# A two-layer decoder segment on one core: the first normalisation is moved behind the projections, and x is also laid out transposed

## The chip, the cores and the metric

The kernel runs on one core of a Trainium2 chip. Its time is the device time of one execution in microseconds; the time before is the median of three runs, 907.67 (907.3 to 909.54). The engines are TensorE (PE; its weight loads are PEld), VectorE (DVE), ScalarE (ACT), GpSimd (POOL) and SyncE (SP, whose queue issues nearly all DMAs). Each engine works through its own instructions in a fixed order, and waits on semaphores for the others.

## The reference

Two layers over 1024 tokens of width 1024, batch 1, all in float32. Each layer is x <- x + RMSNorm(mixer(RMSNorm(x))):

```python
def rmsnorm(x, w):
    y = x * lax.rsqrt(jnp.mean(x * x, axis=-1, keepdims=True) + NORM_EPS)
    return y * w

h = rmsnorm(x, pre_norm_w[0])
proj = h @ w_in + b_in                       # 1024 x 2304: q 1024, k 128, v 128, z 1024
q, k = partial_rope(q, positions), partial_rope(k, positions)
o = sliding_window_gqa(q, k, v, sinks)       # 16 query heads, 2 key heads, window 128
x = x + rmsnorm((o * silu(z)) @ w_out + b_out, post_norm_w[0])
```

Layer 1 has a gated linear recurrence in place of the attention. The change touches only the first RMSNorm and the projections of layer 0. Since the norm's factor r[t] is one number per token, (x * r * w) @ W = r * ((x * w) @ W): the row factor can be applied after the product as well as before it.

## The kernel before

Products are exact to float32 by splitting: a matrix a is held as two fp32r tiles, hi (a rounded copy) and lo (a - hi), and a product is three matmuls, hi hi + hi lo + lo hi (`product`, L186). The tokens stand in two halves of 512, the model width in eight slices k of 128. `act[k, half]` is the pair (acth, actl), 128 x 512, of the transposed normalised input. The weights come in slots of 128 x 512 (`wraw`, 256 KB each, four buffers), are split into `whi` and `wlo` (ten pairs, and two of their own for the key weights, kw) and are freed after their last use.

A projection unit (`proj_feat`, L191) makes one 128-column group of the output for one half: eight k times three matmuls, 24 products of 128 x 512 into one PSUM bank. Layer 0 has units v, k, q (g, ct) and z, each for both halves. The eviction of a unit differs by kind: q is biased, partly rotated, split into qh and ql and stored to DRAM (`qd`), from which attention reads its blocks (`QS`); k is rotated by tables cosT, sinT, cosK and kept as KH, KL; v is transposed; z is gated into og.

The head. Before the branch (the `tc.If` on a flag that tells which form of the recurrence is safe) the first 512 rows of x are loaded as four tiles of 128 tokens, squared on ScalarE (L978), and their row factors made on GpSimd (`rstd_of`, L211). After the branch VectorE multiplies each row by its factor (`norm_rows`), TensorE transposes the result in 128 x 128 pieces (`transpose_half`, L233, four for each k, 32 in all), and ScalarE and VectorE take acth and actl out of PSUM (`act_from_psum`, L177). The second half goes the same way a little later, between the first units. `advance` (L137) splits the weights as slots come free: hi on GpSimd up to slot 19 and on ScalarE after, lo on VectorE, and for slots 2 and 3 on GpSimd.

Then come 16 attention blocks (g, b), into which the remaining units are woven as filler for TensorE by a table of counts (`fill`, `at`). At the end `g_split` splits o * silu(z) into act again, and the output projection `out0_first` follows.

What sets the order: the framework places instructions by priorities (`tc.high_priority`) and a schedule that it makes at build time; instructions of an engine wrapped in `InOrder` keep the order in which they are written. Before, only VectorE is wrapped, and only in the head. In a build's rows such instructions carry the line of `InOrder` (L87).

## Time and profile before

| what | value |
|---|---|
| median of three runs | 907.67 us |
| the profiled execution: its time, its span | 907.38 us, 905.7 us |
| TensorE busy | 883.6 us, 98% |
| VectorE, ScalarE, GpSimd busy | 556.7, 378.2, 330.6 us |
| products of layer 0's input projection that TensorE runs by 59.49 us | 168 |
| DMA moved | 78.63 MB |

The page gives the busy time of each engine, the groups of instructions by line, and the chain of work that ended last. Busy matmul times overlap (a product takes 0.39 us from start to end, while the next starts after 0.23), so TensorE's pace is read from the distance between starts. Views with a time window show single instructions; times are microseconds from the span's start.

### The profile page before, as it was taken

What the parts mean: (1) busy time and instruction counts of PE and PEld (TensorE: products, weight loads), DVE (VectorE), ACT (ScalarE), POOL (GpSimd) and SP (SyncE); (2) the same over time, 40 slices, a digit from 0 to 9 for tenths busy, and PEclk for the clock granted to TensorE, in tenths of its full rate; (3) what the DMA queues carried; (4) which work ended last, traced back from release to release, by engine and by line L of the source; (5) the groups of instructions that cost most, each with busy time, mean ns of one, the idle gap of its engine ahead of it and who ended that gap; (6) DMA issues with size and microseconds to landing.
All of it is one profiled execution on the core that took longest, in us unless ns stands there. A gap on an engine that the chain in (4) does not pass through costs nothing.

```text
span 905.7 us, 14367 instructions
## 1 busy us (share of the span) xinstructions
PE 883.6 (98%) x5342; PEld 738.6 (82%) x5342; DVE 556.7 (61%) x919; ACT 378.2 (42%) x982; POOL 330.6 (37%) x498
## 2 busy tenths in 40 slices
...
GB/s 284 159 146 184 105 184 128 154 56 76 85 37 81 81 93 138 172 122 42 87 50 34 25 47 1 69 58 28 35 47 47 1 1 93 1 110 78 24 185 121
DMA packets 53608, 78.63 MB, mean 87 GB/s; under 512 B 4824, under 2 KB 25048, under 8 KB 53528
## 3 DMA queue, kind: packets, MB, share of 16 engines
...
## 4 chain that ended last, share of the span: by engine, by line
PE 76%; DVE 8%; POOL 6%; issue 5%; ACT 2%; DMA 2%; SPq 0%; POOLq 0%; ACTq 0%; DVEq 0%
PE psmm L189 63%; POOL rstd L217 2%; PE psk L853 1%; PE pso L866 1%; PE pss L530 1%; PE pss L531 1%; PE pso L868 1%; PE pst L551 1%; POOL ms L215 1%; ACT sm L545 1%; DVE actl L180 1%; PE pst L847 1%; PE pst L880 1%; DMA o<-in_x 1%; PE psd L804 1%
## 5 line engine op out<-in xcount | busy, mean ns | idle before, releaser
L189 PE MATMUL psmm<-acth,whi 128*128 128x512 f32 x528 | 208.8, 396 | 0.6 <-DVE ql L378 0.3
L189 PE MATMUL psmm<-acth,wlo 128*128 128x512 f32 x528 | 207.8, 394 | 0.2 <-POOL wlo L155 0.2
L189 PE MATMUL psmm<-actl,whi 128*128 128x512 f32 x528 | 207.7, 393 | 0.0
L189 PE MATMUL psmm<-whi,acth 128*128 128x512 f32 (+1 forms) x520 | 202.7, 391 | 0.5 <-DVE y L632 0.5
L189 PE MATMUL psmm<-wlo,acth 128*128 128x512 f32 (+1 forms) x520 | 200.7, 387 | 0.0
L189 PE MATMUL psmm<-whi,actl 128*128 128x512 f32 (+1 forms) x520 | 200.6, 388 | 0.0
L155 DVE TENSOR_TENSOR wlo<-wraw,whi 128x512 fp32r<-128x512 f32 x126 | 94.8, 765 | 93.4 <-ACT whi L154 86.6
L189 PEld LDWEIGHTS psmm<-acth,whi 128*128 128x128 f32 x528 | 99.3, 188 | 20.9 <-DVE qf L706 0.8
L189 PEld LDWEIGHTS psmm<-acth,wlo 128*128 128x128 f32 x528 | 99.2, 188 | 19.9 <-POOL wlo L155 0.6
L189 PEld LDWEIGHTS psmm<-whi,acth 128*128 128x128 f32 x520 | 97.7, 188 | 20.4 <-DVE y L632 0.8
L189 PEld LDWEIGHTS psmm<-actl,whi 128*128 128x128 f32 x528 | 99.2, 188 | 18.2
L189 PEld LDWEIGHTS psmm<-whi,actl 128*128 128x128 f32 x520 | 97.7, 188 | 19.6
L189 PEld LDWEIGHTS psmm<-wlo,acth 128*128 128x128 f32 x520 | 97.8, 188 | 19.2
L154 ACT ACTIVATE whi<-wraw 128x512 fp32r<-128x512 f32 x112 | 70.2, 631 | 87.3 <-PE psmm L189 67.4
L545 ACT ACTIVATE sm<-sm,st 128x129 f32<-128x129 f32 x128 | 50.0, 393 | 56.0 <-DVE st L543 56.0
L714 POOL TENSOR_SCALAR gate<-gate,lbt 128x512 f32<-128x512 f32 x16 | 17.7, 1108 | 119.1 <-ACT gate L712 108.5
L927 DVE TENSOR_TENSOR y<-psmm,wpost 128x512 f32<-128x512 f32 (+1 forms) x17 | 11.2, 660 | 53.7 <-ACT jk L926 50.5
L217 POOL TENSOR_TENSOR rstd<-ms,nhalf 128x1 f32<-128x1 f32 (+1 forms) x48 | 41.7, 870 | 3.8
L562 POOL TENSOR_SCALAR_AFFINE_SELECT mY<-pT 64x256 fp32r<-64x256 f32 x56 | 28.6, 511 | 36.7 <-ACT pT L554 31.0
L926 ACT ACTIVATE jk<-psmm 128x512 f32<-128x512 f32 (+1 forms) x17 | 9.7, 571 | 67.0 <-PE psmm L189 67.0
L179 ACT ACTIVATE acth<-pst,cst 128x512 fp32r<-128x512 f32 x48 | 29.6, 693 | 12.7 <-PE pst L237 12.7
L565 POOL TENSOR_SCALAR_AFFINE_SELECT mY<-pT 64x256 fp32r<-64x256 f32 x64 | 31.8, 496 | 6.9 <-ACT pT L554 1.6
...
## 6 DMA issues: line engine op xcount, KB each, us to landing
wraw<-in_w SPq DMA_DIRECT2D x132, 256.0 KB
...
```

The source lines that it names most:

```text
L154: nc.scalar.activation(hi, raw, AF.Copy)
L155: W["split_ins"][i] = (nc.gpsimd if on_pool else v).tensor_tensor(lo, raw, hi.bitcast(F32), op=ALU.subtract)
L179: ins = nc.scalar.activation(hi, ps, AF.Copy, scale=scale)
L180: W["actl"][k] = v.scalar_tensor_tensor(lo, ps, scale, hi.bitcast(F32), op0=ALU.mult, op1=ALU.subtract)
L189: W["mm"] = nc.tensor.matmul(ps, a, b, start=(k == 0 and i == 0), stop=(k == NK - 1 and i == 2))
L217: W["rstd"] = keep(nc.gpsimd.tensor_tensor(r, m, nhalf[:, :width], op=ALU.pow))
L545: nc.scalar.activation(sm[:, h, :], sm[:, h, :], AF.Exp, bias=nm[:, h:h + 1], scale=0.125, accum_out=dn[:, h:h + 1])
L562: nc.gpsimd.affine_select(mY[r, :, :64], src[64:, :, :64].bitcast(F32), [[0, 4], [-1, 64]], ALU.is_gt, 0.0, base=0, channel_multiplier=1)
L565: nc.gpsimd.affine_select(mY[r, :, 64:], src[:64, :, 64:].bitcast(F32), [[0, 4], [1, 64]], ALU.is_ge, 0.0, base=0, channel_multiplier=-1)
L714: nc.gpsimd.tensor_scalar(dst, dst, ol, lb, op0=ALU.mult, op1=ALU.add)
L926: nc.scalar.activation(jk[:, c0:c1], ps, AF.Square, scale=D ** -0.5, accum_out=ss)
L927: v.tensor_tensor(y[:, c0:c1], ps, wpost[:, c * 512 + c0:c * 512 + c1], op=ALU.mult)
```

## The change

The host hands over x a second time, transposed (`xt`), so that a tile 128 x 512 of it is one slice k of one half as TensorE needs it.

First half. Each tile of xt is only multiplied by the norm's weight (a factor for each partition) and split: acth on ScalarE, actl on VectorE, both from SBUF. The row factors are left out of the products. The units of this half are therefore unscaled; every eviction of the first half begins with `scaled`: VectorE multiplies the PSUM bank by `rb0`, a 128 x 512 tile that holds the 512 row factors in every partition. `rb0` is made by `spread`: four 128 x 128 transposes of a factor column that is broadcast along the free axis, and a ScalarE copy. The factors come from squares of the ordinary rows of x, which are loaded for that alone, after the first tiles (into the space of the second half's tiles, and, for the second half's rows, of the tables cosT, sinT, cosK and kf/tK).

The first two units, v and q (0, 1), run side by side: for each k three products of the one and three of the other. Their weights (slots 0, 2, 1, 3 in this order) are loaded between the tiles of xt. Of slots 0 and 2 the first 128 columns are split on ScalarE, the rest on GpSimd; all lo parts are VectorE's.

Second half. Its tiles of xt are loaded after the rows of x, multiplied in place by `rb1` (the even k on GpSimd, the odd ones on VectorE), and then split like the others. So its units need no `scaled`.

All five engines are now wrapped in `InOrder` through the head. Further: the identity is made on GpSimd instead of loaded; the half-0 q units of group 0 keep qh and ql in the space of o0; the tag ql has one buffer where it had two; z's th moved to the tag qh.

How the order moves, at three places (names: whi_80 to whi_89 are the ten slots, acth_0_104 is k = 0 of the first half, each further k adds 4 to the last number, acth_1_106 is k = 0 of the second half; kw are the key weights).

TensorE, from the branch on. Before:

```order
L989 COMPARE_AND_BRANCH
L237 MATMUL pst<-cst,o_136 128x128 x24
L189 MATMUL psmm<-acth_0_104,whi_80 128x512
L189 MATMUL psmm<-acth_0_104,whi_82 128x512
L237 MATMUL pst<-cst,o_136 128x128 x4
L189 MATMUL psmm<-actl_0_105,whi_80 128x512
L189 MATMUL psmm<-acth_0_104,wlo_90 128x512
L189 MATMUL psmm<-acth_0_108,whi_80 128x512
L189 MATMUL psmm<-actl_0_105,whi_82 128x512
```

Now:

```order
L1111 COMPARE_AND_BRANCH
L87 MATMUL psmm<-acth_0_104,whi_80 128x512
L87 MATMUL psmm<-actl_0_105,whi_80 128x512
L87 MATMUL psmm<-acth_0_104,wlo_90 128x512
L87 MATMUL psmm<-acth_0_104,whi_82 128x512
L87 MATMUL psmm<-actl_0_105,whi_82 128x512
L87 MATMUL psmm<-acth_0_104,wlo_92 128x512
L87 MATMUL psmm<-acth_0_108,whi_80 128x512
L87 MATMUL psmm<-actl_0_109,whi_80 128x512
```

The 32 transposes of x are gone, and six products for each k stand in a row, two units side by side.

VectorE, where the second half's input is made (sc: a scaled unit; VX: v transposed; xt_206: the second half's tiles; rb_553: rb1). Before, from the scaling of the rows on:

```order
L87 TENSOR_SCALAR xh_329<-xh_329,rstd 128x1024 x4
L155 TENSOR_TENSOR wlo_96<-wraw_102,whi_86 128x512
L155 TENSOR_TENSOR wlo_97<-wraw_103,whi_87 128x512
L378 SCALAR_TENSOR_TENSOR ql<-psmm,cst,qh 128x512
L155 TENSOR_TENSOR wlo_98<-wraw_100,whi_88 128x512
L155 TENSOR_TENSOR wlo_99<-wraw_101,whi_89 128x512
L155 TENSOR_TENSOR kw_213<-wraw_102,kw_212 128x512
L155 TENSOR_TENSOR kw_215<-wraw_103,kw_214 128x512
L180 SCALAR_TENSOR_TENSOR actl_1_111<-pst,cst,acth_1_110 128x512
L180 SCALAR_TENSOR_TENSOR actl_1_115<-pst,cst,acth_1_114 128x512
L180 SCALAR_TENSOR_TENSOR actl_1_123<-pst,cst,acth_1_122 128x512
L466 TENSOR_TENSOR VX<-pst,VX 128x8x64
```

Now, from the last unit of v and q on:

```order
L578 TENSOR_TENSOR VX<-pst,VX 128x8x64
L387 TENSOR_TENSOR sc<-psmm,rb_176 128x512
L453 TENSOR_TENSOR xt_206<-xt_206,rb_553 128x512 x4
L413 TENSOR_TENSOR qtB<-sc,sinT 64x512 x2
L209 SCALAR_TENSOR_TENSOR actl_1_111<-xt_206,cst,acth_1_110 128x512
L209 SCALAR_TENSOR_TENSOR actl_1_107<-xt_206,cst,acth_1_106 128x512
L209 SCALAR_TENSOR_TENSOR actl_1_119<-xt_206,cst,acth_1_118 128x512
L209 SCALAR_TENSOR_TENSOR actl_1_127<-xt_206,cst,acth_1_126 128x512
L414 TENSOR_TENSOR sc<-sc,cosT 128x512
L209 SCALAR_TENSOR_TENSOR actl_1_115<-xt_206,cst,acth_1_114 128x512
L209 SCALAR_TENSOR_TENSOR actl_1_135<-xt_206,cst,acth_1_134 128x512
L209 SCALAR_TENSOR_TENSOR actl_1_123<-xt_206,cst,acth_1_122 128x512
```

The scaling of the rows stood ahead of six weight splits; now it stands behind them, as four multiplies by rb, with the rotation of q (qtB, sc by cosT) among the low parts; the last row shown is the low part of k = 4, the seventh of eight.

TensorE at the end of attention (whi_86 first as the stationary operand: the output projection). Before, the last block:

```order
L189 MATMUL psmm<-actl_0_133,whi_85 128x512
L189 MATMUL psmm<-acth_0_132,wlo_95 128x512
L189 MATMUL psmm<-whi_86,acth_0_104 128x512
L189 MATMUL psmm<-wlo_96,acth_0_104 128x512
L189 MATMUL psmm<-whi_86,acth_0_104 128x512
L189 MATMUL psmm<-wlo_96,acth_0_104 128x512
L573 MATMUL pso<-pT,VX 128x512
L574 MATMUL pso<-pT,VX 128x512
L576 MATMUL pso<-mY,tw 128x4x64
L577 MATMUL pso<-mY,VL 128x4x64
```

Now:

```order
L217 MATMUL psmm<-wlo_99,acth_0_116 128x512
L217 MATMUL psmm<-wlo_98,acth_0_112 128x512
L692 MATMUL pso<-pT,VX 128x512
L693 MATMUL pso<-pT,VX 128x512
L695 MATMUL pso<-mY,tw 128x4x64
L696 MATMUL pso<-mY,VL 128x4x64
L217 MATMUL psmm<-whi_89,actl_0_117 128x512
```

The last attention block (pso with VL) stood behind four products of the output projection; now one such block stands behind 30 of them, and the last one behind 40. From the first transposes of the output projection's result on, TensorE's order is the same in both.

The diff, cut to its core:

```diff
@@ emit @@
+    ac = InOrder(tc, nc.scalar)
+    g = InOrder(tc, nc.gpsimd)
+    pe = InOrder(tc, nc.tensor)
+    sy = InOrder(tc, nc.sync)
+    heads = (v, ac, g, pe, sy)
...
+        FIRST = (0, 2, 1, 3)
...
+        def split_first(i, c0, c1, act=False):
+
+            hi, lo, raw = whi[i][:, c0:c1], wlo[i][:, c0:c1], wraw[i][:, c0:c1]
+            if act:
+                ac.activation(hi, raw, AF.Copy)
+            else:
+                g.tensor_scalar(hi, raw, 1.0, 1.0, op0=ALU.mult, op1=ALU.mult)
+            v.tensor_tensor(lo, raw, hi.bitcast(F32), op=ALU.subtract)
+
+        def split_next():
+            W["split"] += 1
+            i = W["split"] - 1
+            W["place"][i] = W["free"].pop(0)
+            raw, (hi, lo) = wraw[i % NR], W["place"][i]
+            g.tensor_scalar(hi, raw, 1.0, 1.0, op0=ALU.mult, op1=ALU.mult)
+            v.tensor_tensor(lo, raw, hi.bitcast(F32), op=ALU.subtract)
...
-                    on_pool = i in (2, 3)
...
-                    W["split_ins"][i] = (nc.gpsimd if on_pool else v).tensor_tensor(lo, raw, hi.bitcast(F32), op=ALU.subtract)
+                    W["split_ins"][i] = v.tensor_tensor(lo, raw, hi.bitcast(F32), op=ALU.subtract)
...
-        def x_load(xh, half):
-            for j in range(4):
-                t = half * 4 + j
-                for cs in halves(t):
-                    nc.sync.dma_start(xh[:, j, cs], I["x"][t * P:(t + 1) * P, cs])
+        def xt_load(dst, k, half):
+            sy.dma_start(dst[:, k, :], I["xt"][k * P:(k + 1) * P, half * 512:(half + 1) * 512])
@@ layer0 @@
+            rb0 = ka.tile([P, 512], F32, name="rb0")
...
+            def scaled(ps, half, t=None):
+
+                if half:
+                    return ps
+                if t is None:
+                    t = qp.tile([P, 512], F32, tag="th", bufs=2, name="sc")
+                v.tensor_tensor(t, ps, rb0, op=ALU.mult)
+                return t
...
+                    if at is None:
+                        qh = ka.tile([P, 512], F32R, tag="qh", bufs=2, name="qh")
+                        ql = ka.tile([P, 512], F32R, tag="ql", name="ql")
+                    else:
+                        qh, ql = [o0v[:, at + i, :].bitcast(F32R) for i in range(2)]
...
+                xt1 = sp.tile([P, 8, 512], F32, name="xt1")
...
+                rows = [[xt1[:, 2 * j:2 * j + 2, :].rearrange("p a b -> p (a b)") for j in range(4)],
+                        [cosT, sinT, cosK, kft.rearrange("p a b -> p (a b)")]]
+
+                def x_load(j, half):
+                    t = half * 4 + j
+                    sy.dma_start(rows[half][j], I["x"][t * P:(t + 1) * P, :])
+
+                def spread(rs, rb):
+
+                    pt = pp.tile([P, 512], F32, tag="o", name="psr")
+                    for j, r in enumerate(rs):
+                        pe.transpose(pt[:, j * P:(j + 1) * P], r.to_broadcast([P, P]), ident)
+                    ac.activation(rb, pt, AF.Copy)
+
+                def scaled_half(xt, rb, half):
+                    for k in range(NK):
+                        (nc.gpsimd, v)[k % 2].tensor_tensor(xt[:, k, :], xt[:, k, :], rb, op=ALU.mult)
+                        act_from_psum(k, half, xt[:, k, :], cst[:, C_PRE + k:C_PRE + k + 1])
...
-                    for j in range(4):
-                        some()
-                        for cs in halves(j):
-                            norm_rows(sp, o0[:, j, cs], o0[:, j, cs], rs0[j])
-                        hn0.append(o0[:, j, :])
-                    advance(1)
-                    last = transpose_half(hn0, 0, C_PRE, {2: lambda: advance(4)})
...
+                    for k in range(NK):
+                        if k == 6:
+                            split_next()
+                        if k == 0:
+                            act_low(0, 0, o0v[:, 0, :], cst[:, C_PRE:C_PRE + 1])
+                            for i in (0, 2):
+                                split_first(i, 0, P, True)
+                        else:
+                            act_from_psum(k, 0, o0v[:, k, :], cst[:, C_PRE + k:C_PRE + k + 1])
+                        if k in (0, 1):
+                            split_first((0, 2)[k], P, 512)
+                        if k in (2, 3):
+                            split_first((1, 3)[k - 2], 0, 512)
...
+                        if 1 < k < 6:
+                            some(2)
+                        for u in range(2):
+                            c = (k % 4) * P
+                            product(first[u], k, weight(2 * u, k // 4, c, c + P), act[k, 0])
+                            used(2 * u + k // 4)
+                    split_next()
+                    rs0 = []
                     for j in range(4):
...
+                        rs0.append(row_rstd(sp, rows[0][j], jkb))
+                        if j == 1:
+                            split_next()
+                            some(99)
+                    split_next()
+                    cs3 = sines()
                     for j in range(4):
...
+                        x_load(j, 1)
+                        if j % 2:
+                            fetch(NR + 5 + j // 2)
+                    fetch(NR + 8)
+                    split_next()
+                    rs1 = [row_rstd(sp, rows[1][0], jkb)]
+                    ps2 = proj_feat(q_first(0, 2), 0, "s")
+                    spread(rs0, rb0)
+                    store_sines(cs3)
+                    for k in range(NK):
+                        xt_load(xt1, k, 1)
+                    sc = []
+                    for i in range(2):
+                        sc.append(vsc if i == 0 else qp.tile([P, 512], F32, tag="th", bufs=2, name="sc"))
+                        v.tensor_tensor(sc[i], first[i], rb0, op=ALU.mult)
+                    split_next()
+                    rs1 += [row_rstd(sp, rows[1][j], jkb) for j in range(1, 4)]
+                    tables_first()
+                    advance(W_K + 2)
...
+                q_unit(0, 0, 0, at=6)
+                second_tables()
+                with tc.high_priority(offset=1000):
+                    pe.on = True
+                    rb1 = sp.tile([P, 512], F32, name="rb1")
+                    spread(rs1, rb1)
+                    pe.on = False
                 k_unit(0)
+                scaled_half(xt1, rb1, 1)
...
+                        ps = scaled(ps, half)
+                        th = ka.tile([P, 512], F32, tag="qh", bufs=2, name="th")
@@ emit, ahead of the branch @@
-        x_load(o0, 0)
+        o0v = o0.rearrange("p a (b c) -> p (a b) c", b=2)
+        xt_load(o0v, 0, 0)
+        for f in FIRST[:2]:
+            nc.sync.dma_start(wraw[f], I["w"][f])
+        for k in range(1, 4):
+            xt_load(o0v, k, 0)
...
+        nc.gpsimd.memset(ident, 1.0)
+        nc.gpsimd.affine_select(ident, ident, [[1, P]], ALU.is_ge, 0.0, base=0, channel_multiplier=-1)
+        nc.gpsimd.affine_select(ident, ident, [[-1, P]], ALU.is_ge, 0.0, base=0, channel_multiplier=1)
...
+        nc.scalar.activation(act[0, 0][0], o0v[:, 0, :], AF.Copy, scale=cst[:, C_PRE:C_PRE + 1])
         go = nc.values_load(flag[0:1, 0:1])
@@ host_arrays @@
+        "xt": np.ascontiguousarray(np.asarray(x)[0].T),
```

164 lines of the change are left out of this document (83 added, 81 removed).

## The prediction

> **What bounds the kernel now.** I read the page's totals first, then the stretches, then the first 60 us engine by engine.
>
> ```profile
> span 905.7 us, 14367 instructions
> PE 883.6 (98%) x5342; PEld 738.6 (82%) x5342; DVE 556.7 (61%) x919; ACT 378.2 (42%) x982; POOL 330.6 (37%) x498
> ```
>
> ```profile
> 0.00:14.60 14.60, 5.55 (x25) 4.92 (x26) 6.39 (x21) 6.78 (x13) 6.70 (x17) 1.00 0.77 252
> 14.60:59.49 44.89, 44.32 (x213) 36.20 (x213) 36.64 (x66) 21.68 (x36) 19.29 (x32) 1.00 0.60 190
> 60.00:290.00 230.00, 228.60 (x1212) 193.10 (x1211) 190.67 (x355) 151.11 (x454) 144.22 (x249) 1.00 0.38 111
> ```
>
> ```profile
> 290.28 45.52 PE psmm L189 x201
> ```
>
> (A stretch's row: its length, then busy us and instructions of PE, PEld, DVE, ACT, POOL, the granted clock, the DMA share, GB/s.) TensorE is busy almost throughout: its first real product comes at 14.6 us, and from there it hardly pauses. Its pace is 45.52 / 201 = 0.2265 us a 512-column product. So two things can shorten this kernel: an earlier first product, and fewer instructions on TensorE. The change does both, in the head. The second stretch is the yardstick: 213 instructions are the 168 products of seven units (v, four q, k for the first half, k for the second), 40 transposes of x and 4 of v (one more straddles the border). 168 x 0.2265 = 38.1, 44 x 0.11 (next rows) = 4.8, together 42.9 of 44.9 us, so 2.0 us is waiting.
>
> ```profile
> 6.86 0.14 DVE L972 CAST flag<-ld 1x1 int32<-1x1 f32 x1
> 9.42 5.38 PE L237 MATMUL pst<-cst,o 128*128 128x128 f32 x24 [3.09 <-DVE o L87]
> 14.61 1.39 PE L189 MATMUL psmm<-acth,whi 128*128 128x512 f32 x2
> 15.84 0.60 PE L237 MATMUL pst<-cst,o 128*128 128x128 f32 x4
> 31.94 1.47 PE L237 MATMUL pst<-cst,xh 128*128 128x128 f32 x12
> 59.49 0.39 PE L189 MATMUL psmm<-acth,whi 128*128 128x512 f32 x1
> ```
>
> ```profile
> 12.26 0.33 POOLq L984
> 12.86 3.16 POOL whi L152 x4
> ```
>
> The first rows are the timeline (start, length, what, and the idle time before it with what ended it), the last two the chain of waits. The reader sees the old head: the flag for the branch at 7.0, norm and 24 transposes up to 14.6, weights split on POOL only from 12.86.
>
> **The head.** New order: x arrives transposed, one 256 KB tile for each k, and the first product needs only the branch, 128 columns of one split weight and one copied tile. POOL went from reading the flag at 12.26 to work at 12.86, 0.6 us; the flag at 7.0 plus 0.6 is 7.6. A short ACT copy (row below, 0.39 for 129 columns) and 0.2 for the weight load put the first product at 8.2, 6.4 us earlier. The transposed tiles were asked for at the start, and 48 products need 8 tiles and 4 weights, 3.1 MB.
>
> ```profile
> 0.00:10.00 10.00, 0.95 (x4) 0.66 (x5) 2.38 (x10) 5.14 (x8) 2.55 (x11) 1.00 0.79 273
> 10.00:20.00 10.00, 9.72 (x46) 7.94 (x45) 9.41 (x20) 6.24 (x13) 8.71 (x11) 1.00 0.83 290
> L545 ACT ACTIVATE sm<-sm,st 128x129 f32<-128x129 f32 x128 | 50.0, 393 | 56.0 <-DVE st L543 56.0
> ```
>
> At 273 and 290 GB/s 3.1 MB has landed by about 11.3, ahead of what follows. Two things slow the first 48 products (10.9 us at full pace, so 19.1).
>
> One is TensorE's own pace after idling: the 24 transposes take 5.38, (5.38 - 0.42) / 23 = 0.216 each, those at 15.84 (0.60 - 0.27) / 3 = 0.11. Half pace held for up to 6 us. In 6 us 13 products run instead of 26, a loss of up to 3.0. The Trainium skill (TensorE: Matmul & The Clock Gate, Part 1: The HAM clock gate) says the array runs at half its clock until it has been busy for about 3.4 us; by that the loss would be an estimated 1.7, and the trace agrees in kind, with a longer stretch.
>
> The other is VectorE, which now makes every low part in sequence: 8 low parts of x, six weight pieces and eight small steps of the rope tables before the last.
>
> ```profile
> 14.89 2.05 DVE L87 SCALAR_TENSOR_TENSOR actl<-pst,cst,acth 128x512 fp32r<-128x512 f32 x3
> 16.17 2.99 POOL L155 TENSOR_TENSOR wlo<-wraw,whi 128x512 fp32r<-128x512 f32 x2
> 16.87 1.15 DVE L87 TENSOR_TENSOR wlo<-wraw,whi 128x512 fp32r<-128x512 f32 x1
> 17.94 3.37 DVE L87 SCALAR_TENSOR_TENSOR actl<-pst,cst,acth 128x512 fp32r<-128x512 f32 x5
> 23.99 0.66 DVE L87 TENSOR_SCALAR rt<-rt 128x64 f32<-128x64 f32 x3
> 36.44 0.69 DVE L155 TENSOR_TENSOR kw<-wraw,kw 128x512 fp32r<-128x512 f32 x1 [0.75 <-POOL kw L152]
> ```
>
> An actl is 0.67 (3.37 / 5), a weight's low part 0.69 with POOL quiet and 1.15 beside a busy POOL, a rope step 0.2. Low end: 8 x 0.67 + about 3.5 for the weights + 1.6 = 10.5. High end: POOL reads SBUF for some 4 of these 11 us, at 1.15 / 0.69 that is 2.4 more, 12.9. From 7.6 the last low part is out at 18.1 to 20.5, and six products (1.4) follow: 19.5 to 21.9; by the half pace up to 22.1. I take 21.5. That the old actl kept its 0.67 beside POOL at 14.89 does not carry over, because it read PSUM and the new one reads SBUF twice. The Trainium skill (SBUF — State Buffer, Who interferes with whom) says that a VectorE instruction with two SBUF inputs contends with a POOL instruction that reads SBUF; the 1.15 against 0.69 agrees, and by it the high end is the truer one.
>
> **Up to the end of the seventh unit.** 120 more products are 27.2, and 4 transposes of v and 8 that spread the row factors 1.3: 50.0 if nothing waits, against 59.49. That ceiling of 9.5 is 6.4 (start) - 2.4 (head) + 32 x 0.11 = 3.5 (transposes net) + 2.0 (old waits).
>
> ```profile
> 20.48 1.06 ACT L225 ACTIVATE jkx<-xh 128x1024 f32<-128x1024 f32 x1
> 24.36 0.55 POOL L217 TENSOR_TENSOR rstd<-ms,nhalf 128x1 f32<-128x1 f32 x1
> ```
>
> The rows of x for the squares are now loaded as well, 4.2 MB more. The first half's rows are whole after 6.4 MB, by 24 at 290 GB/s; a square (1.2 with its read-out) and a factor (0.8 with the add before it) end at 26, and the spread is wanted at 21.5 + 5.4 = 26.9: no wait, with 1 us to spare. The two evictions that wait for it hold PSUM banks that are wanted again only at 32.8.
>
> The wait I expect is at k of the second half. Its x tiles are scaled only after the second spread: 21.5 + 72 x 0.2265 + 0.9 + 0.4 = 39.1, plus an ACT copy of 0.7: 39.8. TensorE wants the first such tile at 39.1 + 5.4 = 44.6. In VectorE's order there stand, before the low part of k = 4 (the seventh): four scalings, two qtB, one cosT, seven actl, some of it beside four POOL scalings (2.99 / 2 = 1.5 each).
>
> ```profile
> 49.59 1.40 DVE L371 TENSOR_TENSOR qtB<-qf,sinT 64x512 f32<-64x512 f32 x2 [3.12 <-issue]
> 51.02 0.69 DVE L372 TENSOR_TENSOR qf<-qf,cosT 128x512 f32<-128x512 f32 x1
> ```
>
> Low: 4 x 0.61 + 1.4 + 0.7 + 7 x 0.67 = 9.2, so 49.0; high, with 1.15 for the first ones, 12.6: 52.4. Four k (2.7) remain behind it: the unit ends at 51.7 to 55.1 instead of 50.0. I take the middle, 53.4: a gain of 6.1 at this point. The transposed second half (2.1 MB) is behind one weight load that VectorE frees at about 27; even at 290 GB/s it lands by 37, unless the 9.5 MB ahead of it are late (a rival).
>
> **Attention.** Twelve more units of the first half (four q, eight z) pay an extra VectorE multiply out of PSUM.
>
> ```profile
> 300.46 1.28 DVE L632 TENSOR_TENSOR ya<-psmm,bout 128x512 f32<-128x512 f32 x2
> 60.00:80.00 20.00, 19.82 (x101) 16.50 (x100) 18.57 (x32) 10.80 (x30) 4.84 (x7) 1.00 0.51 148
> 100.00:120.00 20.00, 20.00 (x106) 16.99 (x105) 19.65 (x38) 10.82 (x33) 8.65 (x14) 1.00 0.48 141
> 260.00:280.00 20.00, 19.00 (x94) 15.32 (x93) 19.12 (x33) 13.80 (x39) 15.52 (x23) 1.00 0.25 69
> L547 DVE RECIPROCAL st<-st 128x4 f32<-128x4 f32 x32 | 5.6, 176 | 23.8 <-ACT sm L545 23.7
> ```
>
> 12 x 0.64 = 7.7 us. VectorE has 39 us free of 230, most of it (23.7) spent waiting for exponentials, but the stretches at 100 and 260 are full, and there about six of the twelve land: 3.8. Cover is TensorE's filler, products of other units; the new order lets the last attention block come 40 products (9 us) into the output projection, where it came 4 in, so a late attention is partly provided for. I take half, 1.9, with 0 and 7.7 as ends.
>
> ```profile
> 56.79 1.19 SPq L381 DMA_DIRECT2D qd<-ql  x2
> 57.41 2.94 DMA qd<-ql
> ```
>
> The single buffer for ql: a store lands about 4.8 after its ql is written (0.7 + 1.2 of issue + 2.9), under a unit's 5.4; taken as 0.
>
> From the output projection's first transposes on, TensorE's order is unchanged, so what is gained before is kept. Sum against the profiled execution's 907.4 (span 905.7; the median of three is 907.67): 907.4 - 6.1 + 1.9 = 903.2.
>
> **Rivals.**
> - The second half of x is ready in time: VectorE's order costs nothing because the low parts are made while the eight earlier k products run, and attention has cover. Then the ceiling holds: 907.4 - 9.5 = 898. For it: 39 us of free VectorE. Against: seven low parts after 39.8 do not fit before 47.3 at 0.67 each.
> - The other side: VectorE becomes the bound of attention. All 7.7 fall on TensorE, which waits in a fixed order behind each late softmax, and k of the second half ends at 55.1 (gain 4.4): 907.4 - 4.4 + 7.7 = 910.7. It decides from about 4.4 us of exposure. For it: 98% at 100 us. Against: 83% over the whole. With half of this, 3.9, on top of a gain of 4.4: 907, no change.
> - Loads: x is fetched twice. 11.7 MB until the second half is whole, at 290 GB/s 40 us plus the start, 42 instead of 37: the unit ends about 3 us later, 906. For it: 0.83 DMA share already at 10 to 20. Against: SP's queue has no long wait until the one at 27.
> - The change doesn't do what it says: TensorE starts at 8.2 but stands behind VectorE until the old place, because splitting is the true bound: 10.9 + 6 us more, 907.
>
> **How the numbers follow.** Forecast (901 to 905) 0.45; ceiling (898 to 900) 0.22; VectorE fully the bound 0.09, by half 0.14; loads 0.07; head no faster 0.03. About 0.3% (2.7 us) is what a measurement of this kernel can tell from none. Faster, under 904.9: most of the forecast and all of the ceiling, 0.68. Within: 0.23. Slower, over 910.4: 0.09. The range runs from the ceiling, 898, to 908.8, short of the full VectorE case; the likeliest one's own is 901 to 905.
>
> **What would show it.** First product at 8.2 +- 0.7 and the two first units done at 21.5 +- 1.5; half pace in the first 6 us of products. A TensorE gap of 2 to 5 us in the products of k for the second half, released by a VectorE actl. First product of v for the second half at 53 to 55. VectorE over 85% busy between 55 and 285, with TensorE idle there no more than 3.5 (1.4 before). Wrong if the first product comes after 10, if loads end that gap, or if TensorE loses more than 6 us in attention.

## The result and the profile after

The changed kernel takes 922.19 us (median of four, 921.94 to 922.89) against 908.0 for the kernel before (907.3 to 909.54): a ratio of 1.0155, 95% interval 1.0138 to 1.0173. It is slower by 14.2 us, where 903.2 was forecast and 908.8 was the upper end. The profiled execution took 921.94 us.

The page's totals of the changed kernel:

```profile
span 920.1 us, 14329 instructions
PE 884.2 (96%) x5286; PEld 734.7 (80%) x5286; DVE 572.4 (62%) x936; ACT 380.8 (41%) x984; POOL 336.6 (37%) x502
```

TensorE's busy sum is what it was (884.2 against 883.6), although it has fewer instructions, and the span is 14.4 longer. VectorE gained 15.7 us of work. The stretches that were shown of the kernel before (length, then busy us and instructions of PE, PEld, DVE, ACT, POOL, granted clock, DMA share, GB/s):

```profile
0.00:14.60 14.60, 7.93 (x25) 5.63 (x26) 8.20 (x20) 7.29 (x11) 4.72 (x13) 1.00 0.89 296
14.60:59.49 44.89, 40.16 (x175) 31.95 (x174) 38.61 (x67) 24.09 (x40) 25.37 (x40) 0.96 0.78 264
60.00:290.00 230.00, 216.58 (x1125) 180.58 (x1124) 185.53 (x348) 138.38 (x421) 131.97 (x229) 0.99 0.37 106
100.00:120.00 20.00, 16.37 (x82) 13.60 (x81) 17.23 (x35) 11.70 (x39) 10.36 (x18) 0.91 0.23 66
```

From 60 to 290 TensorE starts 1125 instructions where it started 1212. The stretch from 100 to 120 shows it best: 82 where there were 106, with VectorE less busy (17.23) than before (19.65). TensorE's steps of the head in the timeline:

```profile
6.87 0.80 PE L87 MATMUL psmm<-acth,whi 128*128 128x512 f32 x1 [1.70 <-ACT whi L87]
26.17 0.60 PE L87 MATMUL psr<-cst,rstd 128*128 128x128 f32 x4
49.07 0.80 PE L217 MATMUL psmm<-actl,kw 128*128 128x512 f32 x1 [4.74 <-DVE actl L209]
50.94 1.05 PE L217 MATMUL psmm<-acth,kw 128*128 128x512 f32 x2
52.13 0.63 PE L217 MATMUL psmm<-acth,kw 128*128 128x512 f32 x2
55.80 0.39 PE L217 MATMUL psmm<-acth,whi 128*128 128x512 f32 x1
```

These are the first product, the first spread of row factors (behind 72 products), the gap in the products of k for the second half, its recovery, and the first product of v for the second half. That last one stood at 59.49 before, so the head is 3.7 us ahead here. The other end of the stretch that changed is in the second norm: its first `xn` made from y, here before and then after (one made from ya starts 0.7 earlier in both):

```profile
342.58 0.74 DVE L658 SCALAR_TENSOR_TENSOR xn<-y,rstd,wpost 128x512 f32<-128x512 f32 x1
```

```profile
357.21 0.75 DVE L777 SCALAR_TENSOR_TENSOR xn<-y,rstd,wpost 128x512 f32<-128x512 f32 x1
```

From there to the end of the span the two take 563.1 and 562.9 us. Between the two marks the kernel before takes 342.58 - 59.49 = 283.1 and the changed one 357.21 - 55.80 = 301.4. So the whole account is: 3.7 won in the head, 18.3 lost in attention, nothing after. I call that second number, the time between the two marks beyond 283.1, the loss in attention of a kernel. (The stretch also holds the output projection.) In both kernels the first mark is the start of product 169 of the input projection, behind the 168 of seven units. Some of the kernels below weave the products of v into those of k, so in all of them the mark is taken by that count. What TensorE has left behind it, up to the second mark, is then the same in every kernel: 1445 instructions.

Where it is lost the chain of waits tells. Its shares by line from 40 to 140 us, before and then after:

```profile
by line: PE psmm L189 65.0%; PE pss L530 5.5%; PE pss L531 5.3%; PE pst L551 4.4%; DMA QS<-qd 4.2%; DMA qd<-ql 2.9%; PE pso L573 2.1%; DVE actl L180 2.0%; PE pso L574 1.9%; PE pso L577 0.9%; issue 0.9%; PE pso L576 0.7%; ACT kr L425 0.7%; D
```

```profile
by line: DMA qd<-ql 14.2%; issue 8.8%; ACT sm L664 6.4%; DVE KL L546 5.5%; DVE sm L657 4.8%; DVE st L661 4.7%; DVE qtB L413 4.5%; DVE wlo L179 4.3%; DVE pT L674 3.5%; DVE o L698 3.4%; DVE kft L540 2.9%; DVE ql L420 2.9%; ACT KH L545 1.9%; D
```

Before, TensorE's own products are the chain. After, none of them is in the list of the first thirteen: for a hundred microseconds the chain runs through VectorE, instruction behind instruction, and through the stores that free the one ql buffer. A piece of it, and then what TensorE does there:

```profile
80.24 5.21 DMA qd<-ql
85.53 0.75 DVE ql L420
...
103.34 0.04 DVE st L666
...
103.55 0.69 DVE qtB L413
104.25 0.81 DVE qtB L413
...
105.08 0.07 DVE sm L667
...
105.79 0.68 DVE pT L674
106.46 0.60 DVE wlo L179
```

```profile
106.61 0.63 PE L670 MATMUL pst<-cst,sm 128*128 128x128 f32 x4 [1.28 <-DVE pT L674]
109.54 0.50 PE L692 MATMUL pso<-pT,VX 128*128 128x512 f32 x1 [2.30 <-POOL pT L689]
112.78 0.78 PE L217 MATMUL psmm<-acth,whi 128*128 128x512 f32 x1
113.37 0.42 PE L217 MATMUL psmm<-actl,whi 128*128 128x512 f32 x1
```

The softmax has its reciprocal at 103.34. The multiply by it (`sm`, L667) comes at 105.08, behind 1.5 us of q's rotation in VectorE's order. TensorE has run out of other products by then; it waits 1.28 for the transposes of that softmax (what ends this wait is `pT`, VectorE's next instruction, which reads out the transposes before) and 2.30 for its value products, and works at half pace until 113.4. The waits, 60 to 330 us (total, times, longest), TensorE's and VectorE's for the store:

```profile
PE pso L692 <- POOL pT L689: 8.9, 8, 2.3
PE pst L670 <- DVE pT L674: 1.3, 1, 1.3
...
DVE ql L420 <- DMA qd<-ql: 5.6, 4, 2.6
```

Before, the greatest of TensorE's there was this one, and VectorE never waited for the store:

```profile
PE pso L573 <- POOL pT L570: 0.7, 2, 0.5
```

### The profile page after: what moved, and what is told of

Read it like the earlier page. It is cut to its first block, busy times and chain, and to the rows that moved or that the text cites. A ratio compares the mean times of both kernels' runs of the same rounds, so it can differ in the third digit from the quotient of the medians.

```text
span 920.1 us, 14329 instructions
## 1 busy us (share of the span) xinstructions
PE 884.2 (96%) x5286; PEld 734.7 (80%) x5286; DVE 572.4 (62%) x936; ACT 380.8 (41%) x984; POOL 336.6 (37%) x502
## 4 chain that ended last, share of the span: by engine, by line
PE 62%; DVE 15%; POOL 6%; issue 5%; ACT 4%; DMA 2%; ACTq 0%; POOLq 0%; DVEq 0%; SPq 0%
PE psmm L217 53%; ACT sm L664 2%; DMA qd<-ql 2%; POOL rstd L245 2%; PE psk L972 1%; PE pso L985 1%; DVE sm L657 1%; DVE st L661 1%; PE pso L987 1%; DVE wlo L179 1%; DVE pT L674 1%; POOL ms L243 1%; DVE sm L667 1%; PE pst L966 1%; PE pst L999 1%
## 5 line engine op out<-in xcount | busy, mean ns | idle before, releaser
L217 PE MATMUL psmm<-acth,whi 128*128 128x512 f32 x504 | 199.8, 396 | 1.8 <-DVE st L662 1.1
L217 PE MATMUL psmm<-acth,wlo 128*128 128x512 f32 x504 | 198.5, 394 | 0.3 <-DVE wlo L179 0.3
L217 PE MATMUL psmm<-actl,whi 128*128 128x512 f32 x504 | 197.3, 392 | 0.0
L179 DVE TENSOR_TENSOR wlo<-wraw,whi 128x512 fp32r<-128x512 f32 x120 | 88.5, 749 | 91.2 <-ACT whi L178 88.8
L217 PEld LDWEIGHTS psmm<-acth,whi 128*128 128x128 f32 x504 | 95.0, 188 | 21.2 <-DVE st L662 1.3
L217 PEld LDWEIGHTS psmm<-acth,wlo 128*128 128x128 f32 x504 | 94.7, 188 | 20.0 <-DVE wlo L179 1.0
L217 PEld LDWEIGHTS psmm<-actl,whi 128*128 128x128 f32 x504 | 95.0, 188 | 17.7
L1046 DVE TENSOR_TENSOR y<-psmm,wpost 128x512 f32<-128x512 f32 (+1 forms) x17 | 11.2, 660 | 53.7 <-ACT jk L1045 51.6
L245 POOL TENSOR_TENSOR rstd<-ms,nhalf 128x1 f32<-128x1 f32 (+1 forms) x40 | 36.3, 907 | 3.2
L649 PE MATMUL pss<-KH,QS 128*128 128x256 f32 (+1 forms) x128 | 34.2, 294 | 1.0 <-DVE sm L657 1.0
```

The lines of the kernel that those rows point to most:

```text
L179: W["split_ins"][i] = v.tensor_tensor(lo, raw, hi.bitcast(F32), op=ALU.subtract)
L217: W["mm"] = pe.matmul(ps, a, b, start=(k == 0 and i == 0), stop=(k == NK - 1 and i == 2))
L245: W["rstd"] = keep(g.tensor_tensor(r, m, nhalf[:, :width], op=ALU.pow))
L649: nc.tensor.matmul(ps[:, i, :nkk], q, KH[:, g, k0:k0 + nkk], start=True, stop=False)
L1046: v.tensor_tensor(y[:, c0:c1], ps, wpost[:, c * 512 + c0:c * 512 + c1], op=ALU.mult)
```

## The experiments

My theory after the result was this: three things make attention's softmax late, and TensorE's filler then runs out ahead of it: (a) the second half's scaling and splitting on VectorE at 39 to 54 us, which leaves VectorE's work for attention late, (b) the single ql buffer, (c) the twelve multiplies. The rival: the order that is built for attention differs, and any of the edits would do that. The change and 18 further kernels stand in one table; "head" is how much earlier than 59.49 product 169 starts, "attention" the loss defined above. "Old way" for the second half is: rows times their factors on VectorE, 32 transposes on TensorE.

| kernel | what it is | us | ratio to before | head | attention |
|---|---|---|---|---|---|
| the change | | 922.19 | 1.0155 [1.0138, 1.0173] | 3.7 | 18.3 |
| a_nosc | without the twelve multiplies | 924.97 | 1.0195 [1.0178, 1.0212] | 3.5 | 19.4 |
| a_ql2 | two ql buffers | 927.91 | 1.0214 [1.0197, 1.0232] | 1.6 | 22.4 |
| a_head | without both: the head alone | 916.76 | 1.0106 [1.0089, 1.0123] | 2.1 | 10.9 |
| a_fix | second half in VectorE's fixed order | 935.05 | 1.0303 [1.0285, 1.032] | -10.6 | 17.5 |
| h_full | the change, second half the old way | 915.69 | 1.0083 [1.0066, 1.01] | 7.2 | 16.3 |
| h_ql2 | the same, two ql buffers | 915.24 | 1.0092 [1.0072, 1.0113] | 5.2 | 12.4 |
| h_ql2p | the same, last instruction of twelve evictions on GpSimd | 916.66 | 1.0096 [1.0079, 1.0113] | 5.1 | 13.8 |
| h_inpl | h_ql2, multiplies in place in PSUM, transposes earlier | 909.11 | 1.0017 [1.0007, 1.0026] | 4.6 | 4.8 |
| h_head | a_head, second half the old way | 912.71 | 1.0048 [1.0032, 1.0065] | 6.8 | 12.6 |
| h_head2 | the same, order alone | 908.02 | 1.0007 [0.9997, 1.0017] | 6.7 | 11.1 |
| b_ql1 | before with one ql buffer | 923.22 | 1.0177 [1.016, 1.0193] | -1.4 | 11.4 |
| b_ql1p | the same, order alone | 919.83 | 1.0139 [1.0122, 1.0156] | -1.0 | 11.1 |
| b_att | before with one buffer and twelve multiplies | 919.93 | 1.0139 [1.0122, 1.0156] | -0.8 | 11.4 |
| b_mul | before with twelve multiplies | 915.52 | 1.0093 [1.0076, 1.011] | 0.4 | 8.0 |
| b_mulin | the same in place | 913.58 | 1.0072 [1.0055, 1.0088] | 0.5 | 6.6 |
| b_mulE | the first eight of them | 911.4 | 1.0047 [1.0031, 1.0064] | 0.3 | 4.2 |
| b_mulL | the last four of them | 908.09 | 1.0007 [0.9998, 1.0017] | 0.1 | 0.6 |
| b_at | before, order alone | 908.54 | 1.0013 [1.0003, 1.0022] | 0.4 | 1.6 |

Times are medians; head and attention come from one profiled execution each, which for h_head2 was at the top of its runs (906.74 to 911.65) and for b_ql1 lay 3 us under the median. The mark in h_full, as an example of the count (its product 169 is the third of v, woven into k):

```profile
52.25 0.39 PE L217 MATMUL psmm<-acth,wlo 128*128 128x512 f32 x1
```

### The change cut in two: its head alone, its edits in attention alone

a_head takes out of the change the twelve multiplies of q (group 1) and z (`late`), whose row factors it leaves out, and the single buffer; b_att puts both into the kernel before.

```diff
# a_head, against the change
-                if half:
+                if half or late:
-                        ql = ka.tile([P, 512], F32R, tag="ql", name="ql")
+                        ql = ka.tile([P, 512], F32R, tag="ql", bufs=2, name="ql")
# b_att, against before (scaled: a copy times 1 into a tile of the tag th)
+                    if g and not half:
+                        ps = scaled(ps)
-                    ql = ka.tile([P, 512], F32R, tag="ql", bufs=2, name="ql")
+                    ql = ka.tile([P, 512], F32R, tag="ql", bufs=1, name="ql")
+                        if not half:
+                            ps = scaled(ps)
```

> The change with the new head alone: q of group 1 and all z units of the first half are taken as if their row factor were already in (no multiply; the factor is left out of these twelve units), th is back in its old tag and ql has two buffers again. If the attention's additions are the cause, the 3.7 us of the head remain: 904 to 906. If the head and the order of the blocks that follows from it are the cause: 915 or more.

> The kernel before with its own head, but with the attention of the change: twelve first-half units (q of group 1, all z) get one more VectorE instruction out of PSUM (a multiply by 1 instead of the row factors, so the output stays the same), z's th lies in the tag qh, and ql has one buffer. If the 18 us that the change loses between the end of the seventh unit (55.8) and the output projection come from the attention's own additions (extra VectorE work and buffers), this kernel loses them too: 908 + 12 to 18 = 920 to 926. If they come from the new head (another start, another order of the blocks), it stays within 3 us of the kernel before: 908 to 911.

Neither half is harmless: the head alone loses 10.9 in attention although nothing of attention's code differs from before, and attention's edits alone lose 11.4 behind the old head. Together they lose 18.3, not 22.

### The single buffer

b_ql1 sets `bufs=1` for ql in the kernel before, and nothing else (the order that is built for TensorE changes with it, from 124 us on); b_mul gives b_att its second buffer back, and TensorE's order is the same in those two.

> The kernel before with one buffer for ql instead of two, nothing else. In the profile of the change VectorE waits 5.6 us for a ql's store, in four places. If these waits reach TensorE: 911 to 914. If they fall where VectorE has time, as the prediction took it: 907.5 to 909.

> The kernel with its own head and the change's attention (run above at 919.9), but with two buffers for ql. TensorE's order is the same with one and with two buffers here, 3.0 us of work before the value products of the 29th piece included. If the single buffer costs through VectorE's waits for the store (2.8 us there): 916 to 918. If it costs only through the order it makes: the same as that run, 919 to 921.

The single buffer costs 923.22 - 907.67 = 15.6 us alone, with the order that comes with it, which is far beyond either expectation. At one and the same order, beside the multiplies, it costs 919.93 - 915.52 = 4.4. VectorE's waits in b_att, 40 to 330 us:

```profile
DVE ql L385 <- DMA qd<-ql: 6.2, 5, 2.7
DVE ql L382 <- DMA qd<-ql: 3.3, 1, 3.3
```

The chain's shares by line from 40 to 140, of b_att and then of b_mul:

```profile
by line: PE psmm L189 41.5%; DMA qd<-ql 8.7%; issue 5.1%; DVE qtB L378 4.6%; POOL mY L574 3.6%; POOL mY L571 3.5%; DVE ql L382 2.8%; POOL pT L577 2.6%; ACT sm L554 2.6%; DVE sm L547 2.6%; PE pss L540 2.0%; DVE o L588 2.0%; PE pss L539 1.9%;
```

```profile
by line: PE psmm L189 77.0%; PE pss L539 5.2%; PE pss L540 5.1%; PE pst L560 3.9%; PE pso L582 2.1%; PE pso L583 1.9%; DVE actl L180 1.3%; PE pso L586 1.0%; PE pso L585 0.7%; DVE ql L385 0.7%; DVE VX L473 0.6%; PE pst L461 0.4%; issue 0.2%;
```

With one buffer VectorE waits 9.5 us for stores, and the store is on the chain for 8.7 us of these hundred; with two TensorE is the chain. So my zero ("a store lands about 4.8 after its ql is written, under a unit's 5.4") was wrong in its own terms: VectorE does stand behind the store, by up to 3.3 us at a time. The evictions don't come one unit apart. In the kernel before, two pairs of ql writes start 3.0 and 0.6 us apart (at 42.2 and 45.1, at 121.4 and 122.0); in b_ql1 the same pairs are 5.9 and 5.5 apart.

### The multiplies

b_mulin makes the twelve multiplies in place in PSUM; b_mulE keeps the first eight, b_mulL the last four; a_nosc takes the twelve out of the change (it leaves out those row factors).

```diff
# b_mulL, against before
+            def scaled(ps):
+                v.tensor_scalar(ps, ps, 1.0, 1.0, op0=ALU.mult, op1=ALU.mult)
+                return ps
...
+                        if not half and p >= 4:
+                            ps = scaled(ps)
```

> The kernel before with twelve more VectorE instructions out of PSUM, at the same units as in the change, but written in place into the bank (a multiply by 1), with th and ql's two buffers as before. Its order keeps at least 9.5 us of TensorE work between scores and transposes, and 7.3 before the value products, like the kernel before. If the added VectorE work is what costs: the twelve give 8 us, 915 or more. If the cover in the order decides: 908 to 911.

> The kernel before with only the first eight of the twelve in-place multiplies (q of group 1 and z units 0 to 3 of the first half, all done by about 225 us), 5.4 us of VectorE work. If only work inside the full stretch at the end costs: 907.5 to 909. If VectorE work costs wherever it lies, or delays the blocks into a worse end: 911 or more.

> The kernel before with only the last four of the twelve in-place multiplies (z units 4 to 7 of the first half, between about 225 and 290 us). TensorE's order is that of the kernel before, except for nothing: the cover at every piece is the same. 4 x 0.68 = 2.7 us of VectorE work in the stretch that is full. If the full stretch is what the multiplies cost: 3 to 6 more than before, 911 to 914. If it was the order that went with them: 908 to 909.

> The change without the twelve multiplies in attention (the row factor is left out of these units), with ql on one buffer and th in the tag qh as in the change. If the extra VectorE instructions are the cause: 904 to 908. If the buffers are: 915 to 922. If the head's order is: 915 to 922 too, and the kernel with the head alone tells the two apart.

The last four fall into the stretch at 260 us that I had called full, leave TensorE's order as it is up to 280 us, and cost 0.07% (-0.02 to 0.17). The first eight cost 4.2 in attention, and all twelve in place 6.6, between the two expectations, most of it in one wait of TensorE (total, times, longest):

```profile
PE pso L581 <- POOL pT L578: 4.5, 2, 4.0
```

That is not 0.64 a piece. And taking them out of the change gains nothing (924.97, above every expectation for it). With the first eight, and with all twelve, TensorE's order is another one from 112 us on, so these two runs don't separate the work from the order. Only b_mulL does, and there four multiplies on VectorE are nearly free. So the term "12 extra multiplies, half exposed" was the wrong kind of term: what TensorE waits for is a late softmax.

### Order alone

b_at moves one entry of the table by one. h_head2 and b_ql1p change the priority of an eviction (h_head2 one table entry too); the instructions are the same.

```diff
# b_at
-                at = [3, 5, 7, 7, 9, 11, 14, 14, 17, 19, 20, 23, 25, 27, 27]
+                at = [3, 5, 7, 7, 9, 11, 14, 14, 17, 19, 20, 22, 25, 27, 27]
# b_ql1p, against b_ql1; h_head2 has this and 26 for 25 in the table, against h_head
-        HP = 400
+        HP = 550
```

> The kernel before with one number of the table that offers filler to the blocks lowered by one (the twelfth, 23 to 22), so one unit is held back for one block. Same instructions, same buffers, no new wait; the built order of TensorE is the same up to the 24th of the 32 softmax pieces, and then leaves less work between scores and transposes (8.8 and 8.3 us of products and other TensorE work at the 26th and 28th, where 10.8 and 9.3 stood) and 7.1 instead of 9.0 between transposes and the value products of the 27th. If the order alone costs time: 911 to 916, with TensorE's waits between 220 and 290 us. If only added work, buffers or waits cost time: 907 to 909.

> The head alone with the second half made the old way (run above at 912.7), with two of the planner's numbers changed (the priority of evictions 550 instead of 400, the thirteenth entry of the table 26 instead of 25): same work and buffers; TensorE's work before the value products of the 29th piece is 9.0 us instead of 3.4, and between scores and transposes of the 30th 12.0 instead of 6.8. If short cover there is the cause of its 9.6 us of waits between 240 and 300: 904 to 908, faster than the kernel before or the same. If VectorE is late there whatever the order: 911 to 914.

> The kernel before with one ql buffer (run above at 923.2), with the priority of evictions 550 instead of 400: same work and buffer; the shortest cover before the value products is 7.5 us where it was 6.2, and at the last eight pieces no cover between scores and transposes is under 9.7 (8.6 before). If the order is what the single buffer costs: 911 to 916. If the buffer's own waits are: 920 or more.

Order alone moved 1.1, 4.7 and 3.4 us (the ten runs of h_head2 themselves spread over 4.9). So the rival is no fancy, but it does not carry the whole: another order left b_ql1 12 us behind.

### The second half on VectorE, or the old way

a_fix tried to mend the change: all eight scalings on VectorE in a written order, multiplies in place. h_head and h_full make the second half as before.

```diff
# a_fix
-                    for k in range(NK):
-                        (nc.gpsimd, v)[k % 2].tensor_tensor(xt[:, k, :], xt[:, k, :], rb, op=ALU.mult)
-                        act_from_psum(k, half, xt[:, k, :], cst[:, C_PRE + k:C_PRE + k + 1])
+                        v.on = ac.on = True
...
+                                v.tensor_tensor(xt[:, k, :], xt[:, k, :], rb, op=ALU.mult)
# h_head and h_full
+                    transpose_half(rows[half], half, C_PRE)
...
+                        norm_rows(sp, rows[1][j], rows[1][j], rs1[j])
-                    spread(rs1, rb1)
```

> The change with two edits: the second half's eight scalings all on VectorE, each followed by the low part of the k before it and ahead of q's rotation (no GpSimd beside it); and in attention the scaling is written in place into the PSUM bank, th back in its own tag. One ql buffer as in the change. Its order keeps 9.0 us and more between scores and transposes and 7.1 and more before the value products. VectorE needs 8 x (0.69 + 0.74) = 11.4 us from 39.3, so the unit k of the second half ends at 51 to 52 instead of 55.8. If the cover decides: attention loses no more than 3 us, 901 to 905. If the twelve multiplies or the buffer cost by themselves: 914 or more.

> The change's head alone (as in the run at 916.8: no multiplies in attention, so the row factor is left out of q of group 1 and z for the first half; two ql buffers, th in its old tag), but the second half's input is made the old way: its four tiles of rows of x, which are loaded anyway for the squares, are scaled on VectorE (4 x 0.88) and transposed on TensorE (32 x 0.11 = 3.5 us), so the eight scalings by rb1 (1.78 us each beside GpSimd) and the second spread are gone. If VectorE's backlog between 39 and 80 us (38.2 busy of 40 in that run, 32.5 in the kernel before) is what makes the new head lose in the first blocks: the gap at 44 and TensorE's 8.6 us of waits between 60 and 140 go, 903 to 908. If any other head would lose as much, because the order is another: 912 or more.

> The change complete (multiplies by rb0 in attention, one ql buffer, th in the tag qh), but with the second half's input made the old way as in the run above. If VectorE's backlog explains the early loss and the multiplies and the buffer explain the rest: the run above plus 8 to 12, 912 to 918. If the three losses only share one queue and shrink together: 908 to 911.

a_fix failed by its own edit. The written order put the scalings behind k's rotation, which waits for a table (VectorE's timeline), and TensorE waited 18.6 for it:

```profile
53.41 0.69 DVE L543 TENSOR_TENSOR kft<-sc,cosK 128x512 f32<-128x512 f32 x1 [8.19 <-DMA cosK<-csd]
```

The waits of TensorE, 40 to 330 us; the second is the bank that VectorE holds while ql's one buffer is being stored:

```profile
PE psmm L217 <- ACT acth L87: 18.6, 1, 18.6
PE psmm L217 <- DVE ql L420: 5.4, 1, 5.4
```

It says nothing for or against the backlog, but gives the price of a scaling with GpSimd quiet (the view of the tile xt: shortest, median and longest in ns, first and last start):

```profile
L87 DVE TENSOR_TENSOR xt<-xt,rb x8: 682/683/693, 61.2 to 69.7; 128x512 f32<-128x512 f32 x8
```

The old way is better in both: 916.76 to 912.71 without the multiplies, and 922.19 to 915.69 with everything. Though it pays 32 transposes, its head is ahead by 4.7 (of a_head's) and 3.5 (of the change's). In attention it gains 2.0 in the complete kernel and loses 1.7 in the other, so h_head came out on the side of the rival (912 or more). There the stalls only came later: TensorE's time beyond its pace (the distances between starts less the median distance of their kind over all these kernels, added up) goes from 8.5 to 5.6 us between the first mark and 140, 3.0 of it a wait for q out of DRAM, and from 6.0 to 9.4 between 240 and the second mark. h_full has that wait too:

```profile
PE pss L642 <- DMA QS<-qd: 4.5, 1, 4.5
```

### All three taken away

From h_full on, complete kernels: h_ql2 gives ql two buffers, h_ql2p moves the second instruction of an eviction to GpSimd, h_inpl multiplies in place instead, with th in its old tag, and asks for the second half's transposes one unit earlier (ahead of q (0, 0) and not behind it). a_ql2 gives the change itself its second buffer.

```diff
# h_inpl, against h_ql2
-                    t = qp.tile([P, 512], F32, tag="th", bufs=2, name="sc")
+                    t = ps if late else qp.tile([P, 512], F32, tag="th", bufs=2, name="sc")
-                        th = ka.tile([P, 512], F32, tag="qh", bufs=2, name="th")
+                        th = qp.tile([P, 512], F32, tag="th", bufs=2, name="th")
+                scaled_half(xt1, None, 1)
                 q_unit(0, 0, 0, at=6)
                 second_tables()
-                scaled_half(xt1, None, 1)
# a_ql2, against the change; h_ql2, against h_full
-                        ql = ka.tile([P, 512], F32R, tag="ql", name="ql")
+                        ql = ka.tile([P, 512], F32R, tag="ql", bufs=2, name="ql")
+            pos = rb0[:, :64].bitcast(I32)
```

> As the kernel with the old way for the second half, complete, and with two buffers for ql (room made by keeping the positions and v's middle tile in other tiles). If the single buffer costs 4 us beside the multiplies, as between the two kernels with the old head (919.9 and 915.5): 3 to 5 less than the run above. If it was only a matter of the order: the same within 2.

> As the run above, but VectorE does no more per unit than in the kernel before: for the twelve units the last instruction of the eviction (z's product with th, q's low part) goes from VectorE to GpSimd, after ScalarE has added the bias. If the multiplies cost because VectorE is full between 240 and 300 us: 6 to 8 less than the run above, 902 to 907, faster than both kernels. If GpSimd's 1.1 to 1.5 us each make its masks late instead: no gain.

> The change, complete, with one thing given back: the tag ql has two buffers again (the room comes from keeping the positions in rb0 until it is written, and v's middle tile in other places). Nothing is left out. The change is at 922, the kernel before at 908. The order that is built keeps the same short covers as in the change (3.9 us of TensorE work ahead of the value products in one late block, 6 to 9 in the early ones). If the single buffer costs here what it cost when taken alone from the kernel before (15), 907 to 912. If it costs what it cost beside the multiplies at one and the same TensorE order (4.4), 917 to 918. If it costs nothing, as where the second half was made in the old way, 921 to 923; then the loss lies in the work that is late on VectorE and in the order.

> The change's first half with its twelve multiplies, complete, and three causes taken away together: the second half is made in the old way (row factors on the rows, 32 transposes on TensorE), ql has two buffers, and an eviction multiplies in place in PSUM, so that it needs no further tile. Nothing is left out. The old way costs TensorE 32 x 0.11 = 3.5 us, and a wait of about 4 near 34 us, because the rows are scaled late. If the backlog on VectorE at 40 to 80 us, the buffer and the space of the multiplies make the change's loss in attention, 904 to 909. If attention loses all the same, because the order that is built with twelve more VectorE instructions is worse, 910 to 915.

a_ql2 came out above every expectation, at 927.91. Its wait for the store is down to 2.2 us, but its head is 2.1 later (the edit loads the positions elsewhere), and the chain share of TensorE's products from 40 to 140 us is only 25.2%: the second buffer does not bring TensorE back onto the chain. a_ql2 and h_ql2 differ in the second half alone, so they are the clearest test of it: 927.91 and 915.24, and 22.4 and 12.4 in attention. Its greatest waits of TensorE, 40 to 330 us:

```profile
PE psmm L216 <- DVE actl L208: 4.7, 1, 4.7
PE pss L651 <- DMA QS<-qd: 4.0, 1, 4.0
PE pst L672 <- ACT sm L655: 3.0, 1, 3.0
```

h_ql2p gains nothing over h_ql2. h_inpl is at the upper end of the first theory, 909.11, with nothing left out. Its two marks in the timelines:

```profile
54.94 0.39 PE L216 MATMUL psmm<-acth,whi 128*128 128x512 f32 x1
342.83 0.75 DVE L772 SCALAR_TENSOR_TENSOR xn<-y,rstd,wpost 128x512 f32<-128x512 f32 x1
```

Its chain from 40 to 140, and TensorE's greatest waits from 40 to 330:

```profile
by line: PE psmm L216 62.6%; DMA qd<-ql 5.4%; PE pss L645 3.9%; PE pss L644 3.9%; ACT sm L659 2.9%; PE pst L665 2.6%; DVE st L656 2.0%; PE pst L264 1.9%; issue 1.6%; DVE sm L662 1.4%; DVE pT L669 1.2%; PE pso L687 1.2%; PE pso L688 1.2%; PO
```

```profile
PE pso L687 <- POOL pT L684: 2.4, 4, 1.6
PE pss L644 <- DVE sm L652: 1.8, 1, 1.8
```

TensorE is the chain again. Of the change's 14.2 us, 13 are back: 6.5 with the old second half, nothing measurable with the buffer (0.5), 6.1 with the multiplies in place and the transposes a unit earlier (the two were not tried apart). The steps of this ladder hold in this order only, as the same edits elsewhere show. The loss in attention, by kind of head and by what attention carries:

| head | nothing more | one ql buffer | twelve multiplies | both | multiplies in place, two buffers |
|---|---|---|---|---|---|
| before | 0 | 11.4 | 8.0 | 11.4 | 6.6 |
| new, second half the old way | 12.6 | - | 12.4 | 16.3 | 4.8 |
| new, second half as in the change | 10.9 | 19.4 | 22.4 | 18.3 | - |

Two things are read from it. In the change's row, anything that attention carries more costs another 7 to 12; in the row of the old way at most 3.7, and in the row of the kernel before the loss stops at 11.4. And 7 to 13 us go with almost any edit ahead of or in attention, even where the code of attention is untouched. Only variants that stay near the kernel before (b_at, b_mulL, b_mulE) and h_inpl stay under 5.

The place of the loss tells more than its size. This is TensorE's time beyond its pace, less the same in the kernel before, by stretch:

| kernel | first mark to 140 us | 140 to 240 | 240 to second mark |
|---|---|---|---|
| the change | 10.6 | 1.5 | 6.3 |
| a_nosc | 14.8 | 2.0 | 2.7 |
| a_ql2 | 13.6 | 0.8 | 8.2 |
| h_ql2 | 2.5 | 4.0 | 5.9 |
| a_head | 7.4 | 0.5 | 3.1 |
| h_head | 4.5 | 1.5 | 6.5 |
| h_full | 11.2 | 0.9 | 4.2 |
| b_att | 2.3 | 1.2 | 8.0 |
| b_mul | -0.3 | 1.7 | 6.7 |
| h_inpl | 2.0 | 1.4 | 1.5 |

So there are two losses. The early one, 7 to 15 us, is in all four kernels with the change's second half; with everything else equal the old way takes it from 13.6 to 2.5 (a_ql2 to h_ql2), and from 7.4 to 4.5 where attention carries nothing more (a_head to h_head). In h_full, with its one buffer, another early one stands in its place: the wait of 4.5 above, with half pace behind it until 69.3, and 1.5 behind a ql that waits for its store. The late loss, about 3 to 8 us, is in all these rows but the last, with either head. Which feature of the order or of the edits makes it is still open: no run isolated it. I looked at how much of TensorE's other work stands, by the built order and TensorE's pace, between a block's transposes and its value products. The least is 7.3 us before and 7.8 in h_inpl, 6.4 in the change, and 3.0 to 3.9 in a_ql2, h_ql2, h_head, b_mul and b_att; but h_full has about 7, h_ql2p 7.3 and b_ql1p 7.5, and all three lose over 11. So it is no more than a hint. (The chain's shares don't give the size of a loss: from 40 to 140 us TensorE's products hold 52.7% of it in a_head and 29.5% in h_head, which loses less there.)

No kernel beat the one before: h_head2 is level with twelve factors left out, h_inpl 0.17% (0.07 to 0.26) above.

## Why the prediction failed, step by step

**First product at 8.2.** It came at 6.87, earlier than the 0.7 that I allowed: the flag for the branch was ready at 5.84 where it had been at 7.00, which the working did not have. The order of the head and TensorE's half pace after it (to 11.05) were as foreseen, the two first units were done at 20.7 where 21.5 was forecast, and the first spread stood at 26.17 where 26.9 was. This part of the working holds.

**The wait at k of the second half.** Foreseen in its unit and in its cause (a gap of 2 to 5 us, released by an actl of VectorE); measured 4.74. But it stood at the second low part in VectorE's order (k = 0), where I had reckoned with the seventh (k = 4), and behind it there was no wait. Its end was mis-sized: v's first product at 55.80, not 53.4 and outside 51.7 to 55.1, so 3.7 and not 6.1. The terms are VectorE's and GpSimd's rows there:

```profile
39.29 5.81 DVE L453 TENSOR_TENSOR xt<-xt,rb 128x512 f32<-128x512 f32 x4 [0.29 <-ACT rb L449]
39.34 6.89 POOL L453 TENSOR_TENSOR xt<-xt,rb 128x512 f32<-128x512 f32 x4 [0.79 <-ACT rb L449]
45.13 2.36 DVE L413 TENSOR_TENSOR qtB<-sc,sinT 64x512 f32<-64x512 f32 x2
47.60 2.74 DVE L209 SCALAR_TENSOR_TENSOR actl<-xt,cst,acth 128x512 fp32r<-128x512 f32 x4
```

From the factors to the second low part, which TensorE waited for, my prices give 4 x 0.61 + 1.4 + 2 x 0.67 = 5.2, or 7.3 with 1.15 for a scaling. (The high end of 12.6, up to the seventh, is not its rows' sum: with 1.15 for the four scalings they give 11.4.) It took 48.97 - 39.29 = 9.7. The scalings were 5.81 and not 2.4 to 4.6, and the rotation 2.36, not 1.40. The upper end was drawn from a row with less contention than there was to be. Another 1.5 us went into half pace behind the gap (49.07 to 52.1): I had reckoned with half pace behind the first product and forgot it here.

**Attention, 1.9 with 0 and 7.7 as ends.** This step failed, and with it the forecast: 18.3. It priced the change there as VectorE seconds and let TensorE's filler hide half of them. The runs showed three things in its place. VectorE seconds cost next to nothing in the one run where the order stays (b_mulL: four multiplies, 0.6). VectorE's lateness costs, and it did not come from the twelve multiplies (without them the loss is 19.4) but from the second half in the head (10.0 of a_ql2's 22.4 go with it, though only 2.0 of the change's 18.3 and none of a_head's 10.9). The two stretches from 40 to 60 us, before and after, are these:

```profile
40.00:60.00 20.00, 19.71 (x92) 16.03 (x91) 13.93 (x27) 6.37 (x10) 1.66 (x5) 1.00 0.56 179
```

```profile
40.00:60.00 20.00, 15.27 (x62) 11.99 (x61) 19.28 (x25) 8.78 (x13) 9.22 (x10) 0.91 0.57 192
```

VectorE, with 6 us to spare there before, has none now; it comes out of the second half late, and for a hundred microseconds the chain of waits is its own. I had costed the second half only up to the seventh unit and then called the gain kept. And a new order of attention costs by itself: 1 to 5 us where nothing else changed. The bound of 7.7 had no room for either, since both lie outside the sum of the added instructions. How the late loss, 6.3 of the 18.3, divides between order and work stays open.

**"A late attention is partly provided for."** The last block does come 40 products into the output projection, as the order said. It did not help: the waits were at the value products of earlier blocks (8.9 us in eight waits), behind which TensorE stands in its fixed order, two of them with 4 us of half pace behind them.

**The single ql buffer, taken as 0.** Wrong in the kernel before (4.4 at one order, 15.6 with the order that it makes), though giving it back did not mend the change. The usual distance of two units was compared with a store's time; what counts is the shortest distance, and that was 0.6 in the kernel before already.

**"What is gained before is kept."** From the second norm's first row on it was true (563.1 and 562.9), but the gain was gone by then.

**The rivals.** "VectorE becomes the bound of attention" had the right mechanism for the early loss, and 0.09. Its price, all 7.7, was under half of the loss, and the check I gave for it was wrong: I looked for VectorE over 85% busy, and it is at 185.53 / 230 = 81%, less than before's 83%. A late engine need not be a busy one, for it waits for exponentials and stores in between. "Loads" and "the head no faster" did not occur: the gap was released by VectorE.
